# A hybrid conformer block: hand-over to the feed forward re-ordered, its room in two pools, moving operands at another offset, five PSUM banks in the gated linear unit

## The chip, the cores and the metric

The kernel runs on one core of a Trainium2 chip. A core has a tensor engine (PE: it multiplies a moving operand by a stationary one of 128 x 128 that it has loaded before, and writes the result into PSUM), a vector engine (DVE), a scalar engine (ACT, with tables for functions such as sigmoid), a general engine (POOL) and a queue for transfers (SP); ACT and POOL can issue transfers as well. Each engine works through its own queue in order and waits on semaphores for the others. PSUM has eight banks of 128 x 512 float32.

The metric is the device time of one execution in microseconds: the median over the runs shown.

## The reference, cut to what matters

One block over 512 tokens of width 1024, all in float32:

```python
h = rms_norm(x, mix_pre_g)
proj = h @ w_in                    # u_glu, z, xbc, dt_raw and two gates
gates = sigmoid(proj[..., OFF_GATE:] + gate_b);  g_conv, g_ssm = split(gates)
# conformer branch: gated linear unit, causal depthwise conv of 31 taps, layer norm, silu, matmul
v = val * sigmoid(gt);  v = causal_depthwise_conv(v, dw_w, dw_b)
conv_out = silu(layer_norm(v, ln_g, ln_b)) @ pw_w + pw_b
ssm_out = ssd_branch(z, xbc, dt_raw, ...)          # chunked state space branch, 8 groups
mixed = (g_conv * conv_out + g_ssm * ssm_out) @ w_out
x = x + rms_norm(mixed, mix_post_g)
h = rms_norm(x, ffn_pre_g)                         # the hand-over to the feed forward
gt, up = split(h @ w_gate_up)                      # 1024 x 5632
x = x + rms_norm((silu(gt) * up) @ w_down, ffn_post_g)
```

## The kernel before, in words

**Precision.** Each float32 operand is held as two halves, `hi` (rounded to the format fp32r that PE reads) and `lo` (what is left), and each product is three matmuls, hi·hi, lo·hi and hi·lo (`mm3`, L165 to L169). A weight piece of 128 x 1024 comes from memory into a `raw` tile over SP's queue; ACT copies it to `hi`, and DVE subtracts to make `lo` (`w_part`, L131). For every second piece between number 8 and the first ssm gate, ACT writes −hi into `lo` and POOL issues a transfer that adds the weights from memory onto it. `w_get` splits a piece three pieces ahead of its use; `hi` and `lo` have five buffers each, `raw` five. All pieces come in the one list `ORDER`.

**Order of the work.** The program is written in one order, and a planner with a cost model of its own makes from it the order of each engine's queue: an instruction that is ready may be drawn ahead of one that waits. `not_before(a, b)` is an edge that makes the planner place `a` behind `b` on one engine; it costs no semaphore. `tc.issue_after(i)` does that for a whole block. Tiles come from pools with fixed numbers of buffers; a pool opened where another was closed waits for the readers of the tiles that lay there.

**Stages.** (1) Gated linear unit, eight steps `j`, each with two projections `pv` and `pg` of 24 matmuls of 512 columns, evacuated by `gated` (L426); the first three steps run ahead of the input's norm and are scaled behind. Its PSUM tiles come from `mm_tile`, three banks in turn (5, 6, 7), and for step 1 from banks 0 and 1. Ahead of step 3 stands `proj_z0`, four tiles `pz` of 288 columns. The 31 conv taps of each channel block are DVE instructions (L403), which `conv_some(n)` hands out a few at a time, none ahead of the last matmul begun. (2) The state space branch, eight groups. (3) Gates: eight ssm gates `gs`, eight conv gates `gc`, each a projection and a sigmoid; `TAPS_GATE` taps are handed out behind each while any are left. Among the first conv gates the conv's result is turned to token rows and normalised (`ln`), and turned back with a silu on ACT (`ln_back`) for one block of 128 tokens behind each of gates 3 to 6; behind gate 6 it is split into `vhi` and `vlo`. (4) `ppw`: the pointwise matmul, and the mix of the two branches. (5) `tm_wo`: the output projection with tokens as rows, for four blocks `t` of 128 tokens, in eight PSUM banks. (6) The hand-over. For each block `residual(t)` (L913) squares and sums on ACT, multiplies by the post norm's gain on DVE (`mg`), takes the power on POOL, adds the residual into `xr`, and makes a diagonal `dg` of the next norm's factors; `transposed(t)` (L933) turns `xr` to feature rows by 16 matmuls against `dg`, applies the gain (`xg`, half on DVE, half on ACT), and makes halves of the moving operands. (7) The first half of the feed forward, 22 units `u`, by a scheme with seven block products instead of eight: the moving operands are `b11`, `b21`, `b22` and the sums `t1` to `t4`, each with 256 columns; an even block of tokens gives one half of `b11` and `b21`, and the odd block behind it all the others. The weights' forms are `a11`, `a12` (`prep_a`), and `s2`, `s4`, `s1`, `s3`, `a22` (`prep_s`, four additions on DVE in `s1_` and in place in `raw`, then splits by `halve`). `first(u)` is two products into one bank, `second(u)` three, `third(u)` two, each of 12 matmuls. `second` copies the partial sums into `sg` (even units, pool `h2e`) or `f32` (odd units) before it adds onto them. (8) `tm_wd`: the down projection, final norm and store.

**Around the change.** Behind `wo` of block 2, two matmul steps in, stands `transposed(0)` with `prep_a` of units 0 and 1; four steps on `transposed(1)`; within block 3 `prep_a(2)`, `prep_a(3)` and `transposed(2)`; behind all of it `prep_s(0)`, `first(0)`, `first(1)`, `transposed(3)`, `first(2)`, `first(3)`. Two entries in `hold` (the last square and the last `dg` when block 3 begins, those of block 2) keep the splits of units 0, 2 and 3 from running earlier. The pool `pm` at the right end of the memory holds `gpost0`, `xr`, `mg`, `jk` and `dg` as well as `xg`, `t1` and `t2`; when it and the pool of the mixed rows are closed, `f32` and `h2e` come in their place. The moving operands lie in pool `h2p`, which `place_at` begins at `MOV_AT` = 320 bytes (modulo 512); `w2` behind it starts at 0 again.

## Time and profile before

| what | before |
|---|---|
| median of 3 runs | 1072.7 us (1072.07 to 1073.69) |
| the profiled execution, its own time | 1073.46 us |
| its span, first to last instruction | 1071.7 us |
| mean granted TensorE clock | 0.997 |
| PE busy | 1055.1 us, 98% |
| DVE, ACT, POOL busy | 785.9, 593.9, 75.1 us |
| read from memory | 127.71 MB |

A line of the timeline gives the start and the duration in microseconds, the engine, the line of the program, the operation, its tiles (written, then read; numbers left out), its shape and how many were merged, and in brackets the idle time before it with what ended it. Matmuls overlap in the pipeline, so their durations (0.28 for 256 columns) are longer than the distance of their starts. A line of the waits gives who waited for whom, the total, how often, and the longest. A line of the groups gives, behind the bar, busy time and the mean of one in nanoseconds, then idle time before them.

### The profile page before, as it was taken

Reading aid. Unit: us, or ns where it says so; the run is one execution under the profiler, and the core shown is the slowest. Engines: PE = TensorE matmul, PEld = TensorE weight load, DVE = VectorE, ACT = ScalarE, POOL = GpSimd, SP = SyncE. Lnnn points to the kernel's source line nnn. Section 1 sums busy time; section 2 is a strip of 40 time slices with the busy share of each in tenths; the row PEclk is TensorE's granted clock in tenths of the full one; section 3 lists DMA queues with packets and bytes.
Section 4 is the critical chain, followed back from the end, with each engine's and each line's share of the span. In section 5 each row is a group of like instructions: output and inputs, shape, how many; then the busy total and the mean of one; then the engine's idle time right before and its main releaser. Section 6 shows DMA issues by size and latency. Waiting matters only on the chain.

```text
span 1071.7 us, 15135 instructions
## 1 busy us (share of the span) xinstructions
PE 1055.1 (98%) x5897; PEld 918.4 (86%) x5897; DVE 785.9 (73%) x1156; ACT 593.9 (55%) x974; POOL 75.1 (7%) x98
## 2 busy tenths in 40 slices
PE   9999999999999999999999999999999999999997
PEld 7887889888888888888878878879999999988886
DVE  7899895977695979498994365679998788643334
ACT  7657749685859385934322772466554554532222
POOL 1002001110111011100000000000000000000000
PEclk9999999999999999999999999999999999999999
DMA  8476653666436553631133122523343333353202
GB/s 295 129 181 210 144 134 89 170 157 170 105 118 158 159 123 112 170 104 61 46 112 117 60 99 79 187 89 118 121 136 99 99 119 99 119 196 99 98 1 78
DMA packets 37224, 132.94 MB, mean 124 GB/s; under 512 B 4385, under 2 KB 4897, under 8 KB 36129
## 3 DMA queue, kind: packets, MB, share of 16 engines
q1 hardware_dynamic: 28368, 97.31, 27.6%
q0 software_dynamic: 6048, 26.22, 11.8%
q10 hardware_dynamic: 2736, 8.46, 2.2%
q8 instruction: 46, 0.75, 0.3%
q14 instruction: 26, 0.20, 0.1%
HBM read 127.71 MB, written 4.26 MB: 123 GB/s over the span
## 4 chain that ended last, share of the span: by engine, by line
PE 81%; DVE 7%; ACT 5%; DMA 2%; issue 2%; POOL 0%; DVEq 0%; POOLq 0%; ACTq 0%
PE xy L167 4%; PE xy L168 4%; PE xy L169 4%; PE tm_wd L168 4%; PE tm_wd L167 4%; PE tm_wd L169 4%; PE pz L168 3%; PE pz L167 3%; PE pz L169 3%; PE yd L584 3%; PE pso L167 2%; PE pso L168 2%; PE pso L169 2%; PE px L167 2%; PE px L168 2%; PE px L169 2%
## 5 line engine op out<-in xcount | busy, mean ns | idle before, releaser
L133 ACT CAST whi<-raw 128x1024 fp32r<-128x1024 f32 (+2 forms) x135 | 138.0, 1032 | 188.2 <-PE pso L168 44.7
L403 DVE SCALAR_TENSOR_TENSOR a<-v,prm_t,a 128x485 f32<-128x485 f32 (+16 forms) x240 | 179.3, 751 | 9.4 <-ACT a L400 7.0
L139 DVE TENSOR_TENSOR wlo<-raw,whi 128x1024 fp32r<-128x1024 f32 (+3 forms) x101 | 119.9, 1191 | 40.6 <-ACT whi L133 40.5
L167 PE MATMUL tm_wd<-whi,fh 128*128 128x512 f32 x160 | 62.2, 389 | 0.0
L168 PE MATMUL tm_wd<-wlo,fh 128*128 128x512 f32 x160 | 62.2, 389 | 0.0
L169 PE MATMUL tm_wd<-whi,fl 128*128 128x512 f32 x160 | 62.2, 389 | 0.0
L167 PE MATMUL pz<-whi,hhi 128*128 128x512 f32 (+2 forms) x160 | 55.5, 354 | 0.8 <-DVE sg L429 0.8
L168 PE MATMUL pz<-wlo,hhi 128*128 128x512 f32 (+2 forms) x160 | 56.0, 351 | 0.0
L169 PE MATMUL pz<-whi,hlo 128*128 128x512 f32 (+2 forms) x160 | 56.0, 351 | 0.0
L875 DVE TENSOR_TENSOR wlo_g<-raw,whi_g 128x1024 fp32r<-128x1024 f32 x40 | 48.2, 1221 | 9.5 <-ACT whi_g L874 9.5
L874 ACT CAST whi_g<-raw 128x1024 fp32r<-128x1024 f32 x40 | 41.2, 1051 | 23.5 <-issue 9.4
L1085 DVE TENSOR_TENSOR fl<-f,fh 128x512 fp32r<-128x512 f32 x20 | 13.8, 691 | 50.4 <-ACT fh L1084 50.4
L167 PE MATMUL px<-hhi,whi 128*128 128x512 f32 x128 | 50.2, 392 | 0.0
L168 PE MATMUL pso<-yl,whi 128*128 128x512 f32 x128 | 50.1, 391 | 0.0
L169 PE MATMUL pso<-yh,wlo 128*128 128x512 f32 x128 | 50.0, 390 | 0.0
L169 PE MATMUL px<-hhi,wlo 128*128 128x512 f32 x128 | 49.8, 389 | 0.0
L167 PE MATMUL pso<-yh,whi 128*128 128x512 f32 x128 | 49.8, 393 | 0.0
L168 PE MATMUL px<-hlo,whi 128*128 128x512 f32 x128 | 49.8, 389 | 0.0
L137 POOL DMA_DIRECT2D wlo<-in_w x34 | 30.3, 892 | 267.6 <-ACT wlo L136 126.7
L1084 ACT CAST fh<-f 128x512 fp32r<-128x512 f32 x20 | 12.4, 622 | 60.4 <-PE tm_wd L168 60.4
L386 ACT ACTIVATE L<-L,nacs 128x128 f32<-128x128 f32 x128 | 41.1, 394 | 3.4 <-POOL L L380 3.2
L480 DVE SCALAR_TENSOR_TENSOR x<-px,prm_t,x 128x511 f32<-128x511 f32 (+2 forms) x48 | 35.5, 745 | 3.4 <-ACT x L478 3.2
(430 smaller groups left out, 3221.6 us busy)
## 6 DMA issues: line engine op xcount, KB each, us to landing
raw<-in_w SPq DMA_DIRECT2D x177, 512.0 KB, 3.7
wlo<-in_w POOLq DMA_DIRECT2D x34, 512.0 KB, 5.7
L<-scr POOLq DMA_DIRECT2D x8, 1024.0 KB, 5.2
xT<-in_xT SPq DMA_DIRECT2D x8, 256.0 KB, 5.1
xr<-in_x ACTq DMA_DIRECT2D x4, 512.0 KB, 4.2
x2d<-xr ACTq DMA_DIRECT2D x4, 512.0 KB, 2.6
x<-x2d ACTq DMA_DIRECT2D x1, 2048.0 KB, 10.2
gpost<-in_gp ACTq DMA_DIRECT2D x2, 512.0 KB, 8.0
```

Source lines behind the costliest of these rows:

```text
L133: act.copy(hi[:, c], src[:, c])
L137: pool.dma_start(lo[:, c], w[n][:, c].bitcast(F32R), accum_op=ALU.add)
L139: dve.tensor_tensor(out=lo[:, c], in0=src[:, c], in1=hi[:, c].bitcast(F32), op=ALU.subtract)
L167: mark["pe"] = pe.matmul(ps, lh, rh, start=start, stop=False, skip_group_check=more)
L168: pe.matmul(ps, lh, rl, start=False, stop=False, skip_group_check=more)
L169: pe.matmul(ps, ll, rh, start=False, stop=stop, skip_group_check=more)
L386: act.activation(L[:, h, c, :], L[:, h, c, :], AF.Exp, bias=nacs[:, c, HG * g + h : HG * g + h + 1])
L403: return dve.scalar_tensor_tensor(out=va[j][:, d:], in0=vs[j][:, : T - d], scalar=col("dw_w", j * KC + KC - 1 - d), in1=va[j][:, d:], op0= ...
L480: dve.scalar_tensor_tensor(out=a[:, d:], in0=ps[:, : T - d], scalar=col("ssm_w", i * KS + KS - 1 - d), in1=a[:, d:], op0=ALU.mult, op1=ALU ...
L584: pe.matmul(yd[c // 2][:, c % 2, h, :], s["L"][:, h, c, :], s["xdt"][:, c, h, :], start=True, stop=True)
L874: a_ = act.copy(hi, src)
L875: d_ = dve.tensor_tensor(out=lo, in0=src, in1=hi.bitcast(F32), op=ALU.subtract)
```

## The change

In the order of the program:

- Low halves by accumulating transfer are now made up to the first conv gate, instead of the first ssm gate.
- The tiles of the gated linear unit and of `proj_z0` come from five banks in turn (5, 6, 7, 0, 1), step 1 among them.
- Five taps instead of ten are handed out behind each gate.
- Blocks 2 and 3 are turned back together behind conv gate 5, and the split into `vhi` and `vlo` follows there, one gate earlier.
- `gpost0`, `xr`, `mg`, `jk` and `dg` move to a new pool `pb` at the left, behind `w2`; when it is closed, `h2e` opens in its place. `pm` keeps `xg`, `t1` and `t2`.
- `transposed` for an odd block returns the rest of its work (`b22`, `t3`, `t4`) as a function. For block 1 it is called behind `residual(2)`, for block 3 behind the `t2` halves. `t1` is split ahead of `t2`.
- `prep_a(2)`, `prep_a(3)` and `prep_s(0)` stand behind all of `wo` and are held, the additions too, until block 3's last square and `mg`. Unit 0's `s3`/`a22` follow behind block 3's `t2` halves, as do the splits of unit 1.
- PE's order is fixed by edges: `first(0)`, `first(1)`, `first(2)`, the transposes of block 3, `first(3)`; those of blocks 2 and 3 can't be drawn ahead of the matmuls written before them.
- `MOV_AT` is 192 instead of 320.

```diff
-MOV_AT = 320
+MOV_AT = 192
...
-TAPS_GATE = 10
+TAPS_GATE = 5
...
-        if n % DMA_EVERY == DMA_EVERY - 1 and DMA_FROM < n < seq[("gs", 0)] and not after_zz:
+        if n % DMA_EVERY == DMA_EVERY - 1 and DMA_FROM < n < seq[("gc", 0)] and not after_zz:
...
-        pe.matmul(ps, ll, rh, start=False, stop=stop, skip_group_check=more)
+        mark["pe3"] = pe.matmul(ps, ll, rh, start=False, stop=stop, skip_group_check=more)
+        return mark["pe"]
...
-        return psp.tile([P, T], F32, tag=f"bank{first + i % n}", name=name)
+        return psp.tile([P, T], F32, tag=f"bank{(first + i % n) % 8}", name=name)
...
+    def glu_tile(name):
+        return in_turn("glu", 5, 5, name)
...
-            ps = mm_tile(f"pz0_{t}")
+            ps = glu_tile(f"pz0_{t}")
...
-        if j == 1:
-            pv, pg = [yd_tile(n, f"p{n}_1") for n in range(2)]
-        else:
-            pv, pg = mm_tile(f"pv{j}"), mm_tile(f"pg{j}")
+        pv, pg = glu_tile(f"pv{j}"), glu_tile(f"pg{j}")
...
-        if 3 <= i < 7:
-            ln_back(i - 3)
+        for t in ((), (), (), (0,), (1,), (2, 3), (), ())[i]:
+            ln_back(t)
...
-        if i == 6:
+        if i == 5:
...
-    gpost0 = pmp.tile([P, D], F32, bufs=1, name="gpost0")
+    pb = ExitStack()
+    pbp = pb.enter_context(tc.tile_pool(name="pb", bufs=2))
+    gpost0 = pbp.tile([P, D], F32, bufs=1, name="gpost0")
...
-        dve.tensor_tensor(out=s1_, in0=a21, in1=a22, op=ALU.add)
+        sum_ = dve.tensor_tensor(out=s1_, in0=a21, in1=a22, op=ALU.add)
+        if hold:
+            not_before(sum_, hold[1])
...
-        halve(("s3", "a22"), u, rb_, pair_of_tiles())
+        room = pair_of_tiles()
+
+        def last():
+            halve(("s3", "a22"), u, rb_, room)
+
+        if u:
+            last()
+        return last
...
+        last = mark["pe3"]
         for k in range(KB):
             c = slice(k * P, (k + 1) * P)
-            mm3(ps, wh[:, c], wl[:, c], mh[:, k], ml[:, k], start and k == 0, k == KB - 1, not start)
+            m = mm3(ps, wh[:, c], wl[:, c], mh[:, k], ml[:, k], start and k == 0, k == KB - 1, not start)
+            if k == 0 and mark.get("chain"):
+                not_before(m, last)
...
+        if t == 3:
+            hold += [mark["sq"], m]
...
+                m = pe.matmul(pt[:, k, :], xr[:, c], dg, start=True, stop=True)
+                if t >= 2:
+                    not_before(m, mark["pe3"])
+                    mark["pe3"] = m
...
+            if name == "b22":
+                not_before(h_, mark["hi"])
+                not_before(l_, mark["lo"])
+            mark["hi"], mark["lo"] = h_, l_
...
+        halved("t1", t1)
         halved("t2", t2, -1.0)
-        halved("t1", t1)
-        dve.tensor_tensor(out=t1, in0=xg[1], in1=xg[0], op=ALU.subtract)
-        halved("t3", t1)
-        dve.tensor_tensor(out=t2, in0=t2, in1=b21, op=ALU.subtract)
-        halved("b22", xg[1])
-        halved("t4", t2)
+
+        def rest():
+            halved("b22", xg[1])
+            dve.tensor_tensor(out=t1, in0=xg[1], in1=xg[0], op=ALU.subtract)
+            halved("t3", t1)
+            dve.tensor_tensor(out=t2, in0=t2, in1=b21, op=ALU.subtract)
+            halved("t4", t2)
+
+        return rest
...
             residual(t, ps[t])
+            if t == 2:
+                others()
...
-            transposed(1)
-        if (t, k) == (3, 1):
-            hold += [mark["sq"], mark["dg"]]
-            prep_a(2)
-        if (t, k) == (3, 2):
-            prep_a(3)
+            others = transposed(1)
...
-    prep_s(0)
+    prep_a(2)
+    prep_a(3)
+    last_s = prep_s(0)
+    mark["chain"] = True
+    for u in range(3):
+        first(u)
+    rest = transposed(3)
+    pb.close()
+    h2e = h2.enter_context(tc.tile_pool(name="h2e", bufs=2))
+    hold[:] = [mark["hi"], mark["lo"]]
+    last_s()
+    rest()
+    first(3)
+    mark["chain"] = False
+    prep_s(1)
     hold.clear()
-    first(0)
-    first(1)
-    transposed(3)
-    first(2)
-    first(3)
     pm.close()
     mix.close()
...
-    h2e = h2.enter_context(tc.tile_pool(name="h2e", bufs=2, side="right"))
```

More of the change, by code (lines that the diff above doesn't have):

```diff
@@ L906, in product @@
         mh, ml = mov[mn]
+        last = mark["pe3"]
         for k in range(KB):
             c = slice(k * P, (k + 1) * P)
-            mm3(ps, wh[:, c], wl[:, c], mh[:, k], ml[:, k], start and k == 0, k == KB - 1, not start)
+            m = mm3(ps, wh[:, c], wl[:, c], mh[:, k], ml[:, k], start and k == 0, k == KB - 1, not start)
+            if k == 0 and mark.get("chain"):
+                not_before(m, last)
     xrs, xgs = {}, {}
     def residual(t, ps):
-        xr = pmp.tile([P, D], F32, tag="xr", name=f"xr{t}")
+        nonlocal hold
+        xr = pbp.tile([P, D], F32, tag="xr", name=f"xr{t}")
         nc.scalar.dma_start(xr, x[t * P : (t + 1) * P, :])
-        mg = pmp.tile([P, D], F32, tag="mg", bufs=1, name=f"mg{t}")
+        mg = pbp.tile([P, D], F32, tag="mg", bufs=1, name=f"mg{t}")
         ss = []
         for n, c in enumerate(cols2):
-            ss.append(mean_sq(ps[n], pmp, f"a{t}", n))
-            dve.tensor_tensor(out=mg[:, c], in0=ps[n], in1=gpost0[:, c], op=ALU.mult)
+            ss.append(mean_sq(ps[n], pbp, f"a{t}", n))
+            m = dve.tensor_tensor(out=mg[:, c], in0=ps[n], in1=gpost0[:, c], op=ALU.mult)
+        if t == 3:
+            hold += [mark["sq"], m]
         rs = factor(ss, f"a{t}")
@@ L925, in residual @@
             dve.scalar_tensor_tensor(out=xr[:, c], in0=mg[:, c], scalar=rs, in1=xr[:, c], op0=ALU.mult, op1=ALU.add)
-            ss.append(mean_sq(xr[:, c], pmp, f"b{t}", n))
+            ss.append(mean_sq(xr[:, c], pbp, f"b{t}", n))
         rs = factor(ss, f"b{t}")
-        dg = pmp.tile([P, P], F32, tag="dg", name=f"dg{t}")
+        dg = pbp.tile([P, P], F32, tag="dg", name=f"dg{t}")
         mark["dg"] = dve.tensor_scalar(out=dg, in0=ident, scalar1=rs, scalar2=None, op0=ALU.mult)
@@ L940, in transposed @@
             for k in range(KB):
-                pe.matmul(pt[:, k, :], xr[:, (KB * n + k) * P : (KB * n + k + 1) * P], dg, start=True, stop=True)
+                c = slice((KB * n + k) * P, (KB * n + k + 1) * P)
+                m = pe.matmul(pt[:, k, :], xr[:, c], dg, start=True, stop=True)
+                if t >= 2:
+                    not_before(m, mark["pe3"])
+                    mark["pe3"] = m
             tg = dict(tag=f"xg{t}{n}", bufs=1) if t % 2 == 0 else dict(tag=f"xg{n}", bufs=1)
@@ L954, in halved @@
             if sign > 0:
[L955 to L959 removed]
+                h_ = act.copy(hi, src)
+                l_ = dve.tensor_tensor(out=lo, in0=src, in1=hi.bitcast(F32), op=ALU.subtract)
+            else:
+                h_ = act.activation(hi, src, AF.Copy, scale=-1.0)
+                l_ = dve.scalar_tensor_tensor(
                     out=lo, in0=src, scalar=-1.0, in1=hi.bitcast(F32), op0=ALU.mult, op1=ALU.subtract
                 )
+            if name == "b22":
+                not_before(h_, mark["hi"])
+                not_before(l_, mark["lo"])
+            mark["hi"], mark["lo"] = h_, l_
         if t % 2 == 0:
```

4 lines of the change are left out of this document (removed).

## The prediction

> **What bounds the kernel now.** I read the page first, then the list of waits of the tensor engine (PE), then the timeline around each wait, then busy times by stretches.
>
> ```profile
> span 1071.7 us, 15135 instructions
> ...
> PE 1055.1 (98%) x5897; PEld 918.4 (86%) x5897; DVE 785.9 (73%) x1156; ACT 593.9 (55%) x974; POOL 75.1 (7%) x98
> ...
> PE   9999999999999999999999999999999999999997
> ...
> DVE  7899895977695979498994365679998788643334
> ```
>
> PE is the bound from end to end. The change takes no matmul away, so it can pay only by closing holes in PE's row, by a clock that doesn't fall, or by another rate of the matmuls. The waits of PE:
>
> ```profile
> PE v L167 <- ACT sg L1046: 1.7, 1, 1.7
> ...
> PE pg L167 <- DVE v L435: 1.2, 1, 1.2
> PE pyT L636 <- DVE y L548: 1.2, 2, 0.8
> PE xy L167 <- ACT b11h L955: 1.0, 1, 1.0
> PE ppw L167 <- ACT vhi L771: 1.0, 1, 1.0
> PE pz L167 <- DVE sg L429: 0.8, 1, 0.8
> PE xy L168 <- DVE b11l L956: 0.8, 1, 0.8
> ```
>
> Seven holes, 7.7 us. What a hole costs is read better from the starts around it, against the spacing of undisturbed matmuls. In the timeline of PE:
>
> ```profile
> 44.75 0.40 PE L169 MATMUL pz<-whi,hlo 128*128 128x288 f32 x1
> 45.95 0.40 PE L167 MATMUL pz<-whi,hhi 128*128 128x288 f32 x1 [0.80 <-DVE sg L429]
> ...
> 105.06 0.39 PE L169 MATMUL pv<-hhi,wlo 128*128 128x512 f32 x1
> 106.66 0.50 PE L167 MATMUL pg<-hhi,whi 128*128 128x512 f32 x1 [1.21 <-DVE v L435]
> ...
> 622.51 0.39 PE L169 MATMUL pgc<-hhi,wlo 128*128 128x512 f32 x1
> 623.87 0.73 PE L167 MATMUL ppw<-vhi,whi 128*128 128x512 f32 x2 [0.97 <-ACT vhi L771]
> ...
> 716.74 0.40 PE L169 MATMUL tm_wo<-whi,m1l 128*128 128x512 f32 x1
> 718.18 0.39 PE L167 MATMUL xy<-b11h,a01h 128*128 128x256 f32 x1 [1.04 <-ACT b11h L955]
> 718.41 0.40 PE L167 MATMUL xy<-b11h,whi_g 128*128 128x256 f32 x2
> 719.59 0.56 PE L168 MATMUL xy<-b11l,a01h 128*128 128x256 f32 x1 [0.79 <-DVE b11l L956]
> ...
> 736.69 0.28 PE L169 MATMUL v<-t1h,dlo 128*128 128x256 f32 x1
> 738.64 0.39 PE L167 MATMUL v<-b22h,whi_g 128*128 128x256 f32 x1 [1.68 <-ACT sg L1046]
> ```
>
> And the busy times by stretches (columns: stretch, length, then busy time and count of PE, PEld, DVE, ACT, POOL, then granted clock, DMA share, GB/s; the second fence is of PE alone). A count holds two matmuls that began before the stretch, so two are taken off:
>
> ```profile
> 480.00:565.00 85.00, 84.03 (x406) 69.67 (x405) 78.04 (x116) 27.15 (x45) 2.97 (x4) 1.00 0.24 80
> 717.20:743.40 26.20, 22.75 (x174) 22.15 (x175) 24.52 (x41) 16.63 (x35) 1.71 (x2) 0.93 0.32 102
> 719.95:722.94 2.99, 2.99 (x16) 2.99 (x15) 2.56 (x6) 0.96 (x2) 0.85 (x1) 0.50 0.58 174
> 773.52:777.26 3.74, 3.74 (x35) 3.74 (x34) 3.55 (x6) 3.46 (x6) 0.00 (x0) 1.00 0.09 32
> 900.00:945.00 45.00, 45.00 (x384) 44.98 (x383) 27.65 (x44) 21.12 (x36) 0.00 (x0) 1.00 0.29 94
> 165.00:175.00 10.00, 10.00 (x85) 10.00 (x85) 7.80 (x11) 9.90 (x18) 1.04 (x2) 1.00 0.53 134
> ```
> ```profile
> 946.00:1060.00 114.00, 114.00 (x504) 1.00 0.28 97
> ```
>
> Undisturbed spacings: 114.00/502 = 0.227 us for 512 columns, 45.00/382 = 0.118 for 256; for the 288 of `pz` 0.13, between the two. So the holes cost: 45.95 − 44.75 − 0.13 = 1.07; 106.66 − 105.06 − 0.23 = 1.37; 623.87 − 622.51 − 0.23 = 1.13; at the hand-over 718.18 − 716.74 − 0.23 = 1.21 and 719.59 − 718.41 − 0.24 = 0.94 (the 718.41 row is two matmuls); 738.64 − 736.69 − 0.12 = 1.83.
>
> One loss is in no list of waits: right behind the hand-over's holes the granted clock is 0.50 for 3 us. There 14 matmuls took 2.99 us, 0.214 each; at 0.118 they take 1.65, so 1.34 us are lost to the clock. The Trainium skill ("TensorE: Matmul & The Clock Gate", Part 1) has the clock halved only after an idle window of about 3.4 us; the waits ahead of this stretch are 1.04 and 0.79, so here the trace disagrees. By the page the half clock would have another cause and stay, and the sum below would be 1.34 smaller; I go by the trace.
>
> **The change part by part.**
>
> *Five banks in the gated linear unit.* Each new tile takes the bank of the tile five before it instead of three (or two special ones). Both holes wait for a VectorE evacuation: L429 frees the bank of a projection just finished, and at 106.66 the L435 that frees it stands behind conv taps. With five banks those evacuations have two more projections of time, 24 matmuls each, 5.4 us at 0.227. Gain 1.07 + 1.37 = 2.4. What comes late next: VectorE isn't earlier. But after the second hole it runs out of work itself:
>
> ```profile
> 115.30 0.75 DVE L435 SCALAR_TENSOR_TENSOR v<-pv,prm_t,sg 128x512 f32<-128x512 f32 x1 [1.73 <-ACT sg L434]
> ```
>
> It idled 1.73 us, more than the 1.37 that PE gains, so I give nothing back here. Bounds: 1.4 (one hole stays) to 2.4.
>
> *Half the taps per gate, and six weight pieces' low halves (odd ones of 77 to 88) by accumulating transfers.* In this stage VectorE is busy 78.04 of 85 us:
>
> ```profile
> L403 DVE SCALAR_TENSOR_TENSOR a<-v,prm_t,a 128x496 f32<-128x496 f32 (+29 forms) x45 | 32.6, 733 | 0.1
> L139 DVE TENSOR_TENSOR wlo<-raw,whi 128x1024 fp32r<-128x1024 f32 x13 | 15.9, 1226 | 0.3 <-ACT whi L133 0.2
> ```
>
> Six of the thirteen subtractions leave VectorE, 7.4 us; ScalarE gets six copies of about a cast's time, some 6 us, against 85 − 27.15 = 58 us idle; POOL six issues. Taps move from the first four gates to the last four; the total is the same. The only PE holes in the stage are the two `pyT` ones, 1.2 us. The 0.8 one ends with an evacuation (L548) that stands among taps, so it should shrink; the other follows a chain over ScalarE and POOL that the change doesn't shorten. Bounds 0 to 1.2; I take 0.7, near the larger hole. The weights that now come by transfer:
>
> ```profile
> raw<-in_w SPq DMA_DIRECT2D x177, 512.0 KB, 3.7
> wlo<-in_w POOLq DMA_DIRECT2D x34, 512.0 KB, 5.7
> ```
>
> A piece is split three pieces ahead, 3 × 5.4 = 16 us; less two copies of 1 us, 14 us cover a landing of 5.7. If that cover went, one late piece would cost what it exceeds 14 us by. The SP queue keeps its loads, the 3 MB more ride on a DMA share of 0.24.
>
> *Normalised rows handed back a gate earlier.* At the 622.51 hole ScalarE was alternating between sigmoid and silu, with a table load each way:
>
> ```profile
> 617.10 1.28 ACT L698 ACT_TABLE_LOAD   x1
> ...
> 620.40 2.91 ACT L754 ACTIVATE a<-pv,prm_t 128x128 f32<-128x128 f32 x8
> ```
>
> With blocks 2 and 3 together behind gate 5, and the split behind that, the sigmoid of gate 6 (with its load, 617.10 to 619.1) and the load after it no longer stand ahead of the last eight activations: 3.3 us earlier, against a wait of 1.13. Gain 1.1; low end 0, if the planner still puts that sigmoid between. Queued behind the split are gates 6 and 7's sigmoids; the second pw product needs the bank of gate 6 only 5.4 us later.
>
> *The hand-over.* Three losses should go. (a) The first product waited for block 2's operands (1.21 + 0.94), which were late since blocks 1's extra halves stood ahead of block 2's residual on VectorE, and three weight splits ahead of `b11l`. Now `others` comes behind that residual and the splits are held until block 3's `mg`. (b) With these holes the half clock goes, 1.34. (c) The 1.83 wait was for `sg` rows in memory that the `t` tiles of block 3 had held; `h2e` now lies where `xr`, `mg` and `dg` lay, free once block 3 is transposed. Together 5.3. The new order holds PE to three `first` products, block 3's transposes, `first(3)`: behind the transposes only 24 matmuls of cover (2.8 us) instead of 48, with the `t1` product of unit 0 as filler.
>
> What it costs: VectorE was the tight engine here, busy 24.52 of 26.20 us from the end of `wo` to the low half of unit 2's `s2`/`s4`, which PE used 5.5 us after it was done:
>
> ```profile
> 696.61 0.68 DVE L897 TENSOR_TENSOR raw<-s,raw 128x512 f32<-128x512 f32 x1
> ...
> 742.18 1.23 DVE L875 TENSOR_TENSOR wlo_g<-raw,whi_g 128x1024 fp32r<-128x1024 f32 x1 [0.28 <-ACT whi_g L874]
> ```
> ```profile
> 748.90 0.28 PE L167 MATMUL xy<-t2h,whi_g 128*128 128x256 f32 x1
> ```
>
> Work held until after `wo`: unit 0's four additions (4 × 0.6 net; one is shown at 696.61) and two splits (2 × 1.2), 4.8 us; work that now comes before it: `b11l`, `b21l` and one `mg`, 3 × 0.6 = 1.8. So that low half is done 3.0 us later, 746.4, or 744.7 if all of the 1.7 us in which VectorE was idle are used. PE, 5.3 earlier, wants it at 743.6: a wait of 1.1 to 2.8, of which 24 matmuls of the neighbouring products could be drawn forward to hide any part. I take 1.2 given back: hand-over 4.1. Bounds 1.5 (2.8 given back, and 1.0 of new small waits) to 5.9 (0.6 of slowed matmuls beside the holes as well).
>
> *Moving operands at 192 instead of 320.* The trace shows no other offset of these operands, so I bound the 22 × 7 × 12 = 1848 matmuls of 256 columns by what such matmuls did: 3.74/33 = 0.1133 us in one stretch, 10.00/83 = 0.1205 in the other; against 0.1178 that is −8.3 to +5.0 us. The same operands ran at 0.113 and at 0.118, and at 0.118 with `a01` weights from another pool too (no hole within either run), so I take 0, no effect of the address.
>
> Sum: 2.4 + 0.7 + 1.1 + 4.1 = 8.3 us. The profiled execution took 1073.5, so 1065.2 against it; the median of the runs is 1072.7, 0.8 lower, and from it 1064.4.
>
> **The rivals.**
> 1. VectorE gives the whole hand-over back: PE arrives early at unit 2 and 3 and waits there. For it: the 24.52 of 26.20. Against: 5.5 us of lead. Gain 4.2: 1068.5. Chance 0.16.
> 2. The moved operands let the 256-column matmuls run at 0.113: 1064.4 − 8.3 = 1056.1. For it one stretch of 33; against it, that the same tiles do both. 0.05.
> 3. Slower: the moved operands collide with the weights' reads. It decides from 8.3/1848 = 4.5 ns per matmul on, that is from 0.1223 us; at 0.125 it is +13.3 − 8.3, 1077.7. Against: the slowest such rate shown, 0.1205, gives only 1069.4. 0.07.
> 4. POOL's transfers come too late for the gates. The Trainium skill ("SBUF — State Buffer", "SBUF: two separate sides") says descriptors of such transfers can't be written while VectorE holds the port it shares with GpSimd. As rows of this kernel show it, landings of 5.7 against 3.7 us are all that such a lock has cost while VectorE was busy; with 14 us of cover, six pieces would each have to be over 1.4 us beyond it to cancel the gain. Then 1073. 0.03.
>
> **How the numbers follow.** The sum as told has 0.69. Its own range runs from the low ends, 1.4 + 0 + 0 + 1.5 = 2.9 (1069.8), to the high ends, 2.4 + 1.2 + 1.1 + 5.9 = 10.6 (1062.1); the runs of this kernel spread by 1.6 us, which I add below, since a planner's re-ordering elsewhere can close small holes too. Rival 1 lies within that, rivals 2 to 4 outside, so 1060.5 to 1069.6 leaves out about 2 in 10. With such a spread 0.2% (2.1 us) is about what can be told from no change. Faster: nearly all of the first case, rivals 1 and 2, 0.88; slower: rival 3 and a bit of 4, 0.09; same 0.03.
>
> **What would show it.** In the profile after: no `pz` or `pg` wait of PE; the `ppw` wait gone; no stretch at clock 0.50 behind the last `tm_wo`; ScalarE's copies into `sg` right behind block 3's transposes, and no wait at `v<-b22h`; 40 instead of 34 accumulating transfers; 256-column spacing still 0.118 from 900 us on. The prediction is wrong if that spacing moves, if PE waits for `wlo_g` or `dlo` in units 1 to 4, or if the forced order makes PE wait for block 3's `dg`.

## The result and the profile after

| | before | after |
|---|---|---|
| median, 6 runs each | 1073.34 us (1072.07 to 1074.44) | 1069.4 us (1068.0 to 1071.61) |
| ratio, 95% interval | | 0.9966 [0.9953, 0.9979] |
| profiled execution, span | 1071.7 us | 1067.7 us |

The change is 3.9 us faster. 8.3 were forecast. The page after, its span and the busy times, then the waits of PE in total:

```profile
span 1067.7 us, 15144 instructions
...
PE 1049.2 (98%) x5897; PEld 912.1 (85%) x5897; DVE 782.5 (73%) x1150; ACT 594.7 (56%) x978; POOL 79.7 (7%) x104
```
```profile
PE xy L167 <- DVE sg L1067: 2.8, 4, 1.3
PE xy L167 <- DVE f L1067: 1.5, 3, 0.7
...
PE xy L169 <- DVE clo_g L878: 1.2, 1, 1.2
...
PE xy L167 <- DVE mg L937: 0.9, 1, 0.9
PE yd L585 <- DVE L L564: 0.9, 1, 0.9
PE pyT L637 <- DVE y L549: 0.7, 1, 0.7
PE pso L168 <- DVE yl L639: 0.4, 1, 0.4
PE v L169 <- DVE dlo L878: 0.4, 1, 0.4
PE v L167 <- ACT sg L1081: 0.3, 1, 0.3
```

The waits of `pz`, `pg` and `ppw` are gone, and the one for `sg` rows fell from 1.7 to 0.3. New ones have come, nearly all for VectorE: `xy` for L1067, the addition of Y or V to `sg` and `f` (Y is the second product of `first`, V the one with `t1`), 4.3 us in seven waits, `clo_g`, `dlo`, `mg`; and in the gate stage `yd` and `pso`. The hand-over in the timeline of PE, its waits only, and the busy times of its stretches (columns as in the prediction):

```profile
715.74 0.38 PE L167 MATMUL xy<-b11h,a01h 128*128 128x256 f32 x1 [0.88 <-DVE mg L937]
...
729.92 0.35 PE L167 MATMUL xy<-t2h,whi_g 128*128 128x256 f32 x1 [0.79 <-DVE sg L1067]
733.33 0.38 PE L167 MATMUL v<-b22h,whi_g 128*128 128x256 f32 x1 [0.35 <-ACT sg L1081]
736.83 0.38 PE L169 MATMUL v<-t1h,dlo 128*128 128x256 f32 x1 [0.38 <-DVE dlo L878]
740.33 0.36 PE L167 MATMUL xy<-t2h,chi_g 128*128 128x256 f32 x1 [0.71 <-DVE f L1067]
741.97 0.54 PE L169 MATMUL xy<-t2h,clo_g 128*128 128x256 f32 x1 [1.17 <-DVE clo_g L878]
```
```profile
705.00:715.00 10.00, 9.85 (x52) 8.13 (x50) 5.30 (x12) 4.29 (x13) 1.40 (x2) 1.00 0.14 54
715.00:728.00 13.00, 12.26 (x105) 12.27 (x106) 11.58 (x18) 7.09 (x15) 1.72 (x2) 1.00 0.13 44
728.00:742.00 14.00, 10.60 (x84) 9.66 (x83) 13.87 (x25) 11.57 (x21) 0.00 (x0) 1.00 0.24 74
742.05:745.46 3.41, 3.41 (x16) 3.41 (x17) 2.54 (x4) 1.00 (x2) 0.00 (x0) 0.50 0.68 205
760.00:930.00 170.00, 167.01 (x1433) 164.49 (x1432) 147.98 (x222) 91.80 (x150) 0.00 (x0) 1.00 0.36 115
```

VectorE is busy 5.30 of 10 us up to the end of `wo`, then 11.58 of 13, then 13.87 of 14, and in the last of these stretches PE stops five times. The half clock did not go. It now comes at 742.05. And in the long run of 256-column products PE begins 1431 matmuls in 170 us, and before 1420 (its row stands further down), although it is busy for less of that time.

The clearest view is where PE stands in the same work. This table is worked out from the starts of PE's instructions (the start in the kernel before, and the shift of the others against it, us; minus is earlier). Single executions stand up to 1.0 apart behind stages that no edit touched, so it is the differences down a column that are read.

| start of | before | after | five banks (p1) | gates, rows (p2) | hand-over (p3) | address (p4) | p13 |
|---|---|---|---|---|---|---|---|
| first `px` | 112.23 | −1.99 | −2.08 | +0.34 | +0.69 | +0.03 | −2.55 |
| first `pgs` | 494.15 | −1.13 | −1.67 | +0.59 | +0.73 | +0.81 | −2.63 |
| first `tm_wo` | 667.79 | −2.02 | −1.74 | −0.24 | +0.62 | +0.79 | −3.89 |
| last `tm_wo` | 716.74 | −2.28 | −1.74 | −0.25 | +0.37 | +0.78 | −3.23 |
| 48th `xy` | 726.42 | −5.04 | −1.74 | −0.25 | −2.40 | −0.96 | −4.94 |
| 48th `v` | 748.78 | −1.34 | −1.74 | −0.25 | +0.04 | +0.06 | −5.52 |
| 400th `v` | 895.94 | −2.01 | −2.00 | +0.55 | +1.17 | −1.19 | −10.19 |
| last `v` | 943.80 | −3.57 | −2.00 | +0.54 | +1.17 | −2.74 | −12.24 |

In the column "after" PE gains 2.8 us in the hand-over, gives 3.7 back by the 48th `v`, and gains 2.2 more where nothing was foretold.

### The profile page after: what moved, and what is told of

Same layout as the page of the kernel before. It is cut to its first block, busy times and chain, and to the rows that moved or that the text cites. A ratio compares the mean times of both kernels' runs of the same rounds, so it can differ in the third digit from the quotient of the medians.

```text
span 1067.7 us, 15144 instructions
## 1 busy us (share of the span) xinstructions
PE 1049.2 (98%) x5897; PEld 912.1 (85%) x5897; DVE 782.5 (73%) x1150; ACT 594.7 (56%) x978; POOL 79.7 (7%) x104
## 4 chain that ended last, share of the span: by engine, by line
PE 79%; DVE 11%; ACT 4%; issue 3%; DMA 1%; POOL 1%; SPq 0%; DVEq 0%; POOLq 0%; ACTq 0%
PE tm_wd L169 4%; PE tm_wd L167 4%; PE tm_wd L168 4%; PE xy L167 3%; PE xy L169 3%; PE xy L168 3%; PE px L169 2%; PE px L168 2%; PE px L167 2%; PE yd L585 2%; PE pz L168 2%; PE pz L169 2%; PE pso L168 2%; PE pz L167 2%; PE pso L169 2%
## 5 line engine op out<-in xcount | busy, mean ns | idle before, releaser
L407 DVE SCALAR_TENSOR_TENSOR a<-v,prm_t,a 128x511 f32<-128x511 f32 (+16 forms) x240 | 179.6, 752 | 10.0 <-ACT a L404 7.0
L139 DVE TENSOR_TENSOR wlo<-raw,whi 128x1024 fp32r<-128x1024 f32 (+3 forms) x95 | 112.5, 1187 | 39.5 <-ACT whi L133 39.5
L137 POOL DMA_DIRECT2D wlo<-in_w x40 | 35.6, 890 | 329.5 <-ACT wlo L136 162.0
L136 ACT ACTIVATE wlo<-whi 128x1024 fp32r<-128x1024 f32 x40 | 42.3, 1056 | 0.2
```

Of the source, the lines that this page charges most:

```text
L136: act.activation(lo[:, c], hi[:, c].bitcast(F32), AF.Copy, scale=-1.0)
L137: pool.dma_start(lo[:, c], w[n][:, c].bitcast(F32R), accum_op=ALU.add)
L139: dve.tensor_tensor(out=lo[:, c], in0=src[:, c], in1=hi[:, c].bitcast(F32), op=ALU.subtract)
L407: return dve.scalar_tensor_tensor(out=va[j][:, d:], in0=vs[j][:, : T - d], scalar=col("dw_w", j * KC + KC - 1 - d), in1=va[j][:, d:], op0= ...
```

## The experiments

### The parts one by one

p1: the kernel before with `glu_tile` alone.

```diff
+        return in_turn("glu", 5, 5, name)
...
-            ps = mm_tile(f"pz0_{t}")
+            ps = glu_tile(f"pz0_{t}")
```

> The kernel before with only the five PSUM banks of the gated linear unit. Theory A (the sum of the prediction): both holes go and nothing comes back, so the PE runs 2.4 us earlier from the end of the gated linear unit to the end of the span: 1070.3 where the kernel before takes 1072.7. Theory B (from the trace after, where PE is 2.0 us early at the end of this stage and 1.1 to 1.3 us early at the end of the SSD stage): part of it is given back in the SSD stage, where VectorE is now asked for y and wlo earlier than it has them; then PE is about 2.0 us early behind the gated linear unit and 1.0 to 1.3 at the first gate, and the time falls by 1.0 to 1.3 us. If the give-back in the SSD stage is not seen here, it comes from another part of the change.

1071.09 us, ratio 0.9968 [0.9958, 0.9978]. Theory A: PE is 2.1 us early at the first `px` and stays there, but for 0.4. What the changed kernel lost in the state space (SSD) stage, up to the first gate (0.9), is not a cost of this part: p13 has the five banks too and loses nothing (−2.55, −2.63). It goes with the execution: p15, whose code is that of the changed kernel up to the hand-over, loses 0.1 there, and p4, which edits nothing before the feed forward, 0.8.

p2: both edits of the gate stage. p12: the rows alone. p16: taps and transfers alone.

```diff
-TAPS_GATE = 10
+TAPS_GATE = 5
-        ... DMA_FROM < n < seq[("gs", 0)] ...
+        ... DMA_FROM < n < seq[("gc", 0)] ...
...
-        if 3 <= i < 7:
-            ln_back(i - 3)
+        for t in ((), (), (), (0,), (1,), (2, 3), (), ())[i]:
+            ln_back(t)
-        if i == 6:
+        if i == 5:
```

> The kernel before with only the changes of the gate stage: half the taps per gate, six more accumulating transfers, and the normalised rows and the split one gate earlier. Theory A (the sum): 0.7 + 1.1 = 1.8 us faster, PE 0.7 early at the end of the gates and 1.8 early at the first product of wo. Theory B (from the trace after, where the two pyT waits went but new ones of 0.5 to 1.2 us on yd and pso came): nothing at the end of the gates, 1.1 at the ppw hole: 1.1 us faster or less.

> The kernel before with only the normalised rows and the split one gate earlier. The sum has 1.1 us for it: the ppw wait gone, and PE 1.1 us earlier at the first ppw product than the kernel before, from the same point at the first gate. Rival, that the 1.2 us wait on yd and the 0.6 us wait on pso in the gate stage come from this part too and not from the taps and transfers: then they stand in this trace, and PE gains nothing up to ppw.

> The kernel before with only half the taps per gate and six more accumulating transfers. From the difference of the two runs so far (both parts 0.6 us, the rows alone 1.3 us up to the end of wo) this part costs 0.7 us up to wo: the waits of 1.2 us on yd and 0.6 us on pso stand in its trace, in the place of 1.4 us at pyT. The sum had a gain of 0.7.

p2: ratio 0.9998 [0.9986, 1.0009], which leaves out Theory A's 1.8 us; p12: 0.9992 [0.9983, 1.0000], and its trace has neither the `yd` nor the `pso` wait, so its rival falls; p16 has one run, 1074.45, so only its trace is used. From the first `pgs` to the first `tm_wo` PE gains 0.8 in p2; 1.3 in p12, where the start of the first `pgs` is +0.99 and that of the first `tm_wo` −0.31 against the kernel before; and loses 0.4 in p16 (+0.66 to +1.06). The rows are worth a little more than their 1.1, the taps and transfers cost what they were to bring. The timeline of PE in p16, waits of the gate stage:

```profile
511.35 3.76 PE L584 MATMUL yd<-xdt,L 128*128 128x64 f32 x32 [0.86 <-DVE L L563]
542.47 0.50 PE L168 MATMUL pso<-yl,whi 128*128 128x512 f32 x1 [0.46 <-DVE yl L638]
```

With less of that work on VectorE PE is past `pyT` at once, and waits for the next thing in the same chain, `L`, whose multiplication takes VectorE 2.3 us. By starts the two waits cost 1.84 us, and the `pyT` ones that they replace cost 1.39. Whether the taps or the transfers made the difference was not tried apart.

p3: the hand-over alone, with the operands still at 320 (all hunks of the diff from `gpost0` on).

> The kernel before with only the re-ordered hand-over and its two pools, the moving operands still at 320. Theory A (the sum): 4.1 us faster, the holes and the half clock gone, about 1.2 us of small waits back. Theory B (VectorE gives the whole hand-over back, and the half clock comes a little later instead of going): PE is some 3 us early at the end of the first product pair of unit 0, within 0.5 us of the kernel before by the second product of unit 4, there is a stretch at clock 0.50 between 735 and 750 us, and the time is within 0.5 us of the kernel before.

1073.79 us, ratio 0.9999 [0.9990, 1.0008]. Theory B in time: 2.8 us gained by the 48th `xy`, 2.4 of it given back by the 48th `v`. Its waits in the timeline of PE:

```profile
732.56 0.36 PE L167 MATMUL xy<-t2h,whi_g 128*128 128x256 f32 x1 [0.70 <-DVE sg L1067]
736.03 0.39 PE L167 MATMUL v<-b22h,whi_g 128*128 128x256 f32 x1 [0.35 <-ACT sg L1081]
739.47 0.39 PE L169 MATMUL v<-t1h,dlo 128*128 128x256 f32 x1 [0.22 <-DVE dlo L878]
742.96 0.36 PE L167 MATMUL xy<-t2h,chi_g 128*128 128x256 f32 x1 [0.73 <-DVE f L1067]
744.61 0.39 PE L169 MATMUL xy<-t2h,clo_g 128*128 128x256 f32 x1 [1.18 <-DVE clo_g L878]
```

These are the five waits of the changed kernel. The half clock, though, did not come here, against Theory B.

p4: `MOV_AT = 192` alone.

> The kernel before with only the moving operands 128 bytes lower, at 192. Theory A (the sum): the address does nothing, the time within 0.5 us. Theory B (from the trace after, where PE gains 1.5 us between the 400th and the last v product without any hole having gone there): the address lets part of the 256-column matmuls run at 0.113 instead of 0.118 us, and the time falls by about 1.5 us, all of it behind 800 us. Theory C, that the gain there is by the weights' own state and not by the address: no difference here, and a stretch at 0.113 at another place or none.

1070.47 us, ratio 0.9965 [0.9952, 0.9977]: as much as the whole change. Theory A falls; Theory B has the mechanism, with less than half the size. In the stretch from the 120th to the last `v`, 1391 spacings of PE, 1160 are between 109 and 115.5 ns (called fast from here on) in p4, 1102 in the changed kernel, 5 in the kernel before. At 0.118 − 0.1133 us that is 5.4 us for p4; PE is only 3.0 earlier over this stretch (+0.26 to −2.74), since it now waits more for VectorE.

### What holds the hand-over back

p6: the changed kernel without the first hold (`prep_a(2)` and `prep_a(3)` called behind (3,1) and (3,2), as before).

```diff
-        if t == 3:
-            hold += [mark["sq"], m]
```

> The changed kernel without the holds on VectorE's work for units 0, 2 and 3: the splits of units 2 and 3 and the first addition of unit 0 may run before block 3's last product. Theory F (VectorE is idle for some 3 us before the end of wo because that work is held, and lacks these 3 us behind it): the waits of 0.5 to 1.3 us at t2, b22 and s3 of units 0 to 2 go or fall by half, the stretch at clock 0.50 goes with them, and the second product of unit 4 comes 3 us earlier: 1066.5. Theory G (the work then comes ahead of block 2's or 3's operands, which is what the holds are for): the holes come back at the first product or at block 3's transposes, 1069 to 1071.

1068.5 us, ratio 0.9945 [0.9929, 0.9961]. A miss for both. PE is 2.1 us earlier than in the changed kernel at the 48th `v`, but only the first of the five waits went (0.96 to 0.21); the other four are 0.51, 0.47, 0.81 and 1.34, nearly as they were by starts in the changed kernel (0.51, 0.55, 0.88, 1.34), and most of the rest is the half clock, which did not come. p9 adds to p6 the gates' taps and transfers as before and the edit "Y first" of the next section; p10 is p9 with VectorE relieved outright:

```diff
+        if by_dma:
+            act.activation(lo, hi.bitcast(F32), AF.Copy, scale=-1.0)
+            pool.dma_start(lo, w[seq[("gu", 2 * u)]].bitcast(F32R), accum_op=ALU.add)
```

> The changed kernel with the gates' taps and transfers as before, without the holds on VectorE, and with the addition of Y ahead of the next unit's first addition. Theory I (what the runs showed adds up: five banks 2.0, address 3.5, Y first 2.5, rows handed back earlier 1.1, hand-over without holds 1.0): some 10 us under the kernel before, ratio 0.990, and 2 us under the run with banks, address and Y first alone (0.9917). Rival (the re-ordered hand-over is worth nothing in any company): ratio 0.9917 less the 1.1 us of the rows, 0.9907.

> As the run beside it, and VectorE relieved of two subtractions of 1.2 us at the hand-over: the low halves of a11 and a12 of units 2 and 3 come by a negative copy on ScalarE and an accumulating transfer. Theory J (VectorE is what PE waits for from 731 to 743 us): the waits for dlo, f, clo_g there shrink by up to 2.3 us together, 2 us faster than the run beside it. Rival (ScalarE, which has 1.05 us copies to do for the same operands, or the 5.7 us of landing take its place): the same time within 0.5 us, with waits for ScalarE's copies or for wlo_g in the place of VectorE.

p9: 1065.4, ratio 0.9918 [0.9904, 0.9932], so Theory I's 0.990 is left out and its rival's 0.9907 is not; p10: 0.9921 [0.9909, 0.9933]. There Theory J falls, and its rival does not show either: the waits for `dlo`, `t2` and `clo_g` are the same to 0.01 us. Why stands in the busy times of the two stretches, p10:

```profile
715.00:728.00 13.00, 12.82 (x110) 12.82 (x111) 6.45 (x12) 4.53 (x15) 1.10 (x2) 1.00 0.34 102
728.00:742.00 14.00, 11.42 (x87) 10.47 (x87) 14.00 (x24) 10.36 (x18) 0.00 (x0) 0.98 0.16 43
```

VectorE is idle half of the first stretch and full in the second. It has time enough, in the wrong place. (In the changed kernel the first hold's work lies in the first stretch, 11.58 of 13 us, and the idle time ahead of 715 us: 5.30 of 10 us busy there, against 8.93 in p6. The second stretch is as full in both.) What fills the second one is held by the other hold, `hold[:] = [mark["hi"], mark["lo"]]`: unit 0's last split and unit 1's additions and splits wait for block 3's `t2` halves, and VectorE's later work stands behind them. p13 is p9 without that line; p15 is the changed kernel without both holds.

```diff
-    hold[:] = [mark["hi"], mark["lo"]]
```

> The combined version without the second hold: unit 0's last split and unit 1's additions and splits no longer have to wait for block 3's t2 halves. In the combined run VectorE was busy 5.89 of 13 us from 715 to 728 and 14.00 of 14 from 728 to 742, with 3.5 us of waits of PE in the second stretch. Theory M (the second hold puts the work into the wrong stretch): the waits at b22, dlo, t2 and clo_g between 731 and 743 fall from 3.1 us (0.51, 0.47, 0.81, 1.34) to under 1, and the time falls by 2 to 3 us: 1062.5 to 1063.5. Rival N (the chain behind block 3's transposes sets it: its operands over VectorE and ScalarE, then the sg room): the waits stay within 0.5 us of what they were.

> The changed kernel without either hold and with nothing else changed. Theory M: 2 to 3 us below the run without the first hold (1068.5), so 1065.5 to 1066.5, and the hand-over is then worth what the prediction had for it, 3 to 4 us. Rival N: 1068.5.

p13: 1061.36 us, ratio 0.9897 [0.9884, 0.9911], 2.3 us under p9 by the ratios, little more than the noise. Theory M. Its busy times and waits:

```profile
715.00:728.00 13.00, 11.98 (x105) 11.98 (x106) 12.10 (x21) 5.55 (x10) 1.71 (x2) 1.00 0.41 142
728.00:742.00 14.00, 12.81 (x106) 12.20 (x105) 13.32 (x24) 11.36 (x26) 0.00 (x0) 1.00 0.36 121
```
```profile
716.02 0.38 PE L167 MATMUL xy<-b11h,a01h 128*128 128x256 f32 x1 [2.12 <-DVE mg L936]
729.75 0.51 PE L167 MATMUL v<-t1h,dhi 128*128 128x256 f32 x2 [0.66 <-ACT t1h L974]
730.79 0.39 PE L168 MATMUL v<-t1l,dhi 128*128 128x256 f32 x1 [0.53 <-DVE t1l L975]
```

VectorE now does more in the first stretch (12.10 of 13 us, against 5.89 in p9), and all four waits between 731 and 743 are gone. The price is a wait of 2.1 us at the first product, where block 3's `mg` now comes later (1.0 in p9), and two of 1.2 in all at unit 0's `t1`. So PE gains only 1.0 us on p9 from the last `tm_wo` to the 48th `v` in the two traces; 1.6 more come behind it, where p13 has 1057 fast spacings and p9 702. p15: 1067.95, ratio 0.9956 [0.9944, 0.9968], no better than p6. The four waits are gone there too (PE is 2.7 us earlier than in the changed kernel at the 48th `v`), but the first product cost 2.3 us by starts, the half clock followed at 717.42, and waits for Y took part of the rest (by starts 0.86, 1.41 and 0.81 us, from 783.4, 842.8 and 864.0 on; PE is 1.6 us earlier at the last `v`). So M holds for the waits; for the time it is not shown. No run lifts the second hold and keeps the first.

p14 is the combination without any of the re-ordered hand-over.

> The kernel before with the five banks, the address, Y first and the rows handed back a gate earlier, and with the hand-over as it was: the combined version without the re-ordered hand-over. If that hand-over with its second hold is worth nothing, the time is that of the combined run, 1065.4 (ratio 0.9918); if it is worth the 1 us that lifting the first hold seemed to give, 1066.4.

1065.22 us, ratio 0.9939 [0.9923, 0.9954]. Against p13 the hand-over, once without holds, is worth 0.0042, 4.5 us, give or take 2.2, near what the prediction had for it. In the two traces it is only 1.6 us (from the last `tm_wo` to the 48th `v` PE gains 2.29 in p13, 0.72 in p14); that execution of p14, its fastest of 1062.49 to 1068.38, had no half clock. With the second hold it is not told from nothing (p9 0.9918 and p14 0.9939 are 2.3 us apart, and their intervals overlap).

### The address, and the addition of Y

p5: the changed kernel back at 320. p7: five banks and 192 alone. p11: the kernel before at 64.

> The changed kernel with the moving operands back at 320. Theory D (from the part alone, which ran 3.5 us faster behind the hand-over): the address sets the spacing of the 256-column matmuls; back at 320 fewer than 300 of the 1390 behind the 120th v product keep 0.113 us, the time is 3 us above that of the changed kernel, about 1071.5 to 1072.5, 1.5 to 2 us under the kernel before, which is the gated linear unit alone. Theory E (the rate comes from the holes and where they fall, and the address only went along with it): at least 700 of them still run at 0.113 us and the time is that of the changed kernel, 1069.5.

> The kernel before with two parts only, the five banks and the moving operands at 192; hand-over and gates as before. Theory D (the two parts add up, the rest of the change is worth nothing or less): 2.0 + 3.5 us faster than before, 5.5 in all, and 1.5 to 2 us faster than the changed kernel: ratio 0.9949. Rival (they share a limit, VectorE's additions or the loads in the units of the feed forward, at which an earlier PE waits): 3.7 us, ratio 0.9966, as the changed kernel.

> The kernel before with only the moving operands 256 bytes lower, at 64. In the traces so far 5 to 469 of the 1390 matmuls behind the 120th v product ran at 0.113 us with the operands at 320, and 781 to 1205 with them at 192. Theory K (192 is a good place, or 320 a bad one, among several): at 64 the count falls in one of these two groups, clearly. Theory L (the spacing is set by where the holes fall, and any move shifts them): a count between, 500 to 750. A time of 1074.4 goes with the first group, 1070.5 with the second.

p5: 1071.99, ratio 0.9970 [0.9958, 0.9983], hardly above the changed kernel's 0.9966 as Theory E has it, and 469 fast spacings in its trace, between the theories. p7: 0.9946 [0.9934, 0.9958], Theory D, 2.4 us under p1 and 2.1 under the changed kernel: two parts do at least as well as all of them (the intervals just overlap). p11: 0.9999 [0.9989, 1.0009], so 64 is no better than 320, the time of Theory K's first group; its trace, of the fastest of ten executions, has 605 fast spacings, the count of Theory L. p5 left it open whether the address is worth anything in company, and in p16, at 320, 752 spacings were fast. What PE waits for in these units is seen near 844 us of the changed kernel; VectorE, then PE:

```profile
844.77 0.69 DVE L898 TENSOR_TENSOR s<-raw 128x512 f32<-128x512 f32 x1 [1.18 <-DMA raw<-in_w]
845.38 0.42 DVE L1067 TENSOR_TENSOR sg<-xy,sg 128x256 f32<-128x256 f32 x1
```
```profile
844.26 0.28 PE L169 MATMUL xy<-t4h,wlo_g 128*128 128x256 f32 x1
845.85 0.39 PE L167 MATMUL xy<-t2h,chi_g 128*128 128x256 f32 x1 [1.31 <-DVE sg L1067]
```

VectorE stands 1.18 us for a weight load, to add two blocks of a later unit's weights, and the addition of Y that PE waits for stands behind it in its order. p8 puts it ahead, on p7; p18 does that on the kernel before, and p17 is p13 back at 320.

```diff
-        add(dst[0][:, c1], Y[u])
+        y_ = add(dst[0][:, c1], Y[u])
+        if u >= EARLY_U and u + 1 in sums:
+            not_before(sums[u + 1], y_)
```

> The five banks and 192 as in the run beside it, and from unit 4 on the first addition of the next unit's weights is held until the addition of Y of this unit, so that VectorE doesn't stand waiting for a weight load with the addition of Y behind it. Theory H (the 1.4 us wait at t2 near 845 us is that order, and the ones of 0.2 to 0.5 us behind it too): these waits go, 1.5 to 2 us faster than the run beside it. Rival (the weights are then prepared too late): new waits for wlo_g or clo_g of the next unit, no gain or slower.

> The kernel before with the addition of Y ahead of the next unit's first addition and nothing else. In the kernel before PE is at 0.118 us and waits little for that addition behind 755 us (about 2.7 us over all its stalls, some 10 in number, against 4.8 with the address at 192). Theory H (the order caps only a PE that is faster): 1 to 2 us faster, ratio 0.998 to 0.999. Rival (the stalls themselves throw the spacing back to 0.118 us, whatever the address): with the stalls gone most matmuls run at 0.113, and the time falls by 5 us or more, ratio 0.995.

> The combined version without either hold, with the moving operands back at 320. Theory D (the address sets the odds of the fast spacing, and what it was worth in the changed kernel was eaten by waits for the addition of Y, which are gone here): fewer than 500 of the 1391 matmuls at 0.113 us, against 1057, and 3 to 4 us slower: ratio 0.993 against 0.9897. Theory L (the spacing is chosen at each wait, whatever the address): counts as with 192, and the same ratio within 0.0015.

p8: 1066.39, ratio 0.9917 [0.9903, 0.9931], 3.1 us under p7; the eight waits for Y from 765 us on, by starts 3.4 us in p7, are two of 0.2. Theory H, and more than it said. p18: 0.9975 [0.9965, 0.9985], 2.7 us, so that order held up the slow PE as well, by more than Theory H had; no spacing of 1391 became fast, and the rival falls. p17: 1067.04, ratio 0.9929 [0.9916, 0.9941]: theory D. The same stretch in the kernel before, then p13, then p17:

```profile
760.00:930.00 170.00, 169.65 (x1422) 167.90 (x1421) 144.27 (x216) 89.46 (x147) 0.00 (x0) 1.00 0.35 112
```
```profile
760.00:930.00 170.00, 169.85 (x1479) 169.13 (x1478) 144.29 (x218) 91.94 (x151) 0.00 (x0) 1.00 0.33 111
```
```profile
760.00:930.00 170.00, 170.00 (x1439) 169.46 (x1438) 143.30 (x215) 90.54 (x148) 0.00 (x0) 1.00 0.32 104
```

PE is busy all the time in p17 and still begins 40 matmuls fewer than in p13, 1437 against 1477: 0.1183 us each against 0.1151. By spacings, 1057 of 1391 are fast in p13 and none in p17. So the address does set the spacing, and it is worth 0.0032, 3.4 us, give or take 2.0, where little else stops PE. Within a trace the spacing changes where PE is held up and holds in between: of 69 changes between stretches of eight or more, 67 stand at one to three longer spacings, mostly by 0.2 us or more in sum. At 320 such a stall leaves a fast stretch behind only at times: with few of them (p17, p18) there is no fast spacing at all, and in the seven kernels with more, 4 to 752. At 192 there are 702 to 1205 in ten kernels.

## Why the prediction was wrong

The direction was right and the range held the time, but the change is worth less than half of what was forecast. Two terms that were out by their whole size, with opposite signs, made it look nearer than it was: that the range held the time, 0.2 us inside its end, is luck, since by the trace after 2.0 us came from the address, which the prediction put at 0. That end, 1069.6, is also 0.2 under the prediction's own sum of low ends, 1069.8.

- *Five banks, −2.4*: right. Both holes went; the part alone measured 3.4 [2.4, 4.5], its trace 2.1 at the first `px`. VectorE gave nothing back for it.
- *Taps and transfers, −0.7*: wrong, +0.4 in the trace of p16. Of the 1.2 us of `pyT` waits for `y` 0.4 stood at 301.7 us, in the SSD stage, where none of these edits acts and where p16 still has it; the gate stage had 0.8, and 0.2 behind the chain over ScalarE and POOL. The step that failed is "it should shrink" for the larger one: it did, and what is late next was not named. It is `L`, from the same VectorE, 2.3 us long.
- *Rows and split a gate earlier, −1.1*: right; 1.3 in the trace of p12.
- *Hand-over, −4.1*: wrong; 0 ± 1.0 alone. Losses (a) and (c) did go, for the most part (1.21 + 0.94 to 1.05 by starts, 1.83 to 0.51). The step that failed is "What it costs", 1.2 given back. It counted only the work held until `mg`, and took unit 2's low half as the one operand that would be late. Not counted was the second hold, which puts unit 0's last split and unit 1's additions and splits behind block 3's `t2` halves, into a stretch where VectorE is then full (13.87 of 14 us), while it stood idle for nearly half of the 10 us ahead of 715. PE waited 4.2 us by starts, five times, in units 0 and 1. Rival 1 had this, VectorE giving the whole hand-over back, with 0.16, though it looked for it at units 2 and 3. Taking away the first hold, the one the prediction spoke of, left four of the five waits; taking away the second as well took all four, for a longer wait at the first product. How much of the time is the second hold's alone stays open.
- *(b), "with these holes the half clock goes"*: wrong in the changed kernel, where it came back 22 us later, right behind the last two of the five waits (0.71 and 1.17 us).
- *Address, 0*: wrong; 3.8 alone, 3.4 in p13 against p17. The step that failed is "The same operands ran at 0.113 and at 0.118 … so I take 0". One stretch of 33 fast matmuls, which stood right behind a stall of PE (772.06 us), was read as the spacing that these addresses have. Rival 2 had the mechanism, at 8.3 us, and 0.05. In the changed kernel 1102 fast spacings are 5.2 us, and PE gains 2.0 over that stretch (−1.58 at the 120th `v` to −3.57 at the last): most of the rest went into stalls of PE, above all waits for the addition of Y; by starts its stalls there sum to 2.7 us in the kernel before and to 5.6 in the changed one.
- *"What would show it"*: of the six signs, no `pz`, `pg` and `ppw` wait, 40 accumulating transfers and the `sg` copies were there, though 0.35 us of the wait at `v<-b22h` stayed; the 0.50 stretch had moved; the spacing from 900 us on had changed. And PE waited for `dlo` and for `clo_g`, the low half of `s2`, in unit 1; a wait for `dlo` was a sign that the prediction had against itself.

In sum, by the trace after: banks −2.0, +0.9 lost in the SSD stage, gates and rows −0.9, `wo` −0.3, hand-over +0.7 to the 120th `v` (−2.28 to −1.58), address less its waits −2.0; that is −3.6, against 3.9 measured. The +0.9 is not from the banks and goes with the execution, as p13, p15 and p4 show.

## What to carry to other kernels

A re-ordering that freed the tensor engine here did not pay as long as the vector engine's work was held back from where that engine was idle: compare its busy time in the stretch ahead of the hole and in the one behind it, and read every edge that holds work back, not only the first. When an operand's address changes, count spacings of undisturbed matmuls over a long stretch before calling it free; a fast stretch right behind a wait says little. An instruction that stands waiting for a load (1.18 us here) blocks what stands behind it in its engine's order; putting the addition first was worth 2.7 us beside slow matmuls and 3.1 beside faster ones.

The version p13 (five banks, 192, rows a gate earlier, re-ordered hand-over without holds, Y first, the gates' taps and transfers as before) beats both kernels: 0.9897 [0.9884, 0.9911] of the kernel before, 1061.36 us.

## What the runs showed of the chip that was not expected

*A moving operand's offset sets the spacing of matmuls.* The 22 units' operands begun 320 or 192 bytes into their pool, all else in its place (p17, p13): 0.118 against mostly 0.113 us for 256 columns. Not every other offset does it: 64 gave no gain in time. What in the offset does it, and why a wait can change the spacing of all that follows up to the next one, no run here shows.

*The half clock goes by a grid.* All 14 stretches at clock 0.50 ahead of PE's last matmul, in the 20 traces, start a whole number of 3.413 us after PE's clock first became full, and last 3.413 us (one lasts two). Ahead of 13 of them PE was idle for 1.60 to 2.14 us within the 3.413 us (1.60 in p11, 1.74 in p8, the others 1.81 and more). Windows of the grid without one behind them had up to 1.68, one in p13 1.81, and one at the end of PE's work in p7 1.89. So no sharp bound shows: between 1.6 and 1.9 us of idle it went both ways. A wait costs more or less by where it falls on the grid. The window ahead of the half clock in the changed kernel, and then two of p3, where the last two of the same five waits fell into one each:

```profile
738.64:742.05 3.41, 1.53 (x12) 1.16 (x10) 3.41 (x7) 3.28 (x6) 0.00 (x0) 1.00 0.00 0
```
```profile
739.58:742.99 3.41, 2.68 (x23) 2.51 (x23) 3.41 (x8) 3.04 (x5) 0.00 (x0) 1.00 0.00 0
742.99:746.40 3.41, 2.23 (x16) 1.90 (x16) 3.41 (x5) 1.92 (x6) 0.00 (x0) 1.00 0.08 24
```

Busy 1.53 of 3.41 us brought it; 2.68 and 2.23 did not. The Trainium skill ("TensorE: Matmul & The Clock Gate", Part 1) has a free-running window of 3413 ns, and with that the traces agree; that it takes an idle window does not hold here, about half of one was enough. One stretch (p5, 511.74 us) followed after only 0.86 us of idle and is not explained.
